# A transformer block on one core: weight splits in short steps, compressed logits joined to the window's, gates kept as inverses

## The chip, the cores and the metric

The kernel runs on one core of a Trainium2 chip. The metric is the device time of one execution in microseconds (us). A core has TensorE (PE in the profile), VectorE (DVE), ScalarE (ACT), GpSimd (POOL) and SyncE (SP), which issues most DMAs; POOL issues others. Each engine works through its own list of instructions in a fixed order, and semaphores tie the lists together.

## The reference

One block on x of 1024 positions by 1024 features, all in float32. Cut to what matters here:

```python
u = rms_norm(h, g_norm_mix)
proj = u @ w_in + b_in            # mLSTM q, k, v, o, i, f; NSA q, 6 x kv, gates; merge gates
y_m = mlstm_mixer(...)            # 4 heads of 128, chunks of 128
# NSA: 8 heads of 64 in 2 groups, queries in blocks
kc_, vc_ = compress(k_c, 0), compress(v_c, 1)          # 63 compressed keys and values per group
p_c = masked_softmax(q @ kc_.T + bias_c, cmp_end <= t)
p_s = masked_softmax(q @ k_sel.T + bias_s, mask_s)     # 16 blocks of 64: here all of them
p_w = masked_softmax(q @ k_win.T + bias_w, window 512)
y_n = gate_c * (p_c @ vc_) + gate_s * (p_s @ v_sel) + gate_w * (p_w @ v_win)
mixed = sum(sigmoid(merge) * einsum('btnw,nwd->btnd', [y_m, y_n], w_branch))
h = h + mixed @ w_out
h = h + (silu(f @ w_gate) * (f @ w_up)) @ w_down       # f = rms_norm(h, g_norm_ffn)
out = rms_norm(h, g_final)
```

With 1024 positions the 16 selected blocks are all blocks, so the selected branch is causal attention over all keys. The gates are the sigmoids of three columns per head.

## The kernel before, in words

A float32 product is made of three PE matmuls on a high and a low part of each factor (`mm3`, L269 to L272): high times high (L270), weight low times input high or the reverse (L271, L272). A tensor is split by ACT, which writes the rounded high part, and by DVE or POOL, which writes the difference, the low part. `Stream.split` (L236 to L251) does that for a weight tile of 128 x 8 x 128: ACT's copy is L247, the subtraction L249, on POOL where `pool` is set, else on DVE.

The program runs in stages. Up to about 80 us the input is normalised and transposed and the first projections are made. From there to about 318 the mLSTM runs beside dense projections. From 318 to 382 the query projections of NSA are made (`b2_dense`), two halves to a tile: ACT evicts a half (L846, `snq`), DVE rounds it (L847, `hnq`) and takes the low part (L848, `lnq`), and SP writes both to memory (L850, L851, `d_qh` and `d_ql`). Beside them `compress` makes the 63 compressed keys and values per group; its weights are loaded at L877 (SP), its features come from DVE (L883), its matmuls are L887. After the first query tile `load_pair(0)` has POOL load the queries of a pair of heads (L810, L811) and the keys of a group in high and low parts (L818 to L821: `KH`, `KL`, index 1 for the window's, 0 for the selected keys), 128 x 1024 each, and SP the bias tables `FB`, `FW`.

From 382 to 707 the attention runs in 32 units: 4 pairs of heads by 8 blocks of 128 query rows, in the order 0, 7, 1, 6, 2, 5, 3, 4 of the blocks i. A unit has five logit jobs (`s_job`, L942): window of head 0 and 1 ("w"), compressed of both heads ("c"), selected of head 0 and 1 ("s"). A job takes one of two PSUM buffers S, runs its matmuls with the queries as weights (L974, L975; for "c" L960, L961 with 8i + 8 columns), then DVE adds the bias and keeps the row maximum (L987, with a readout into `nx`), which frees the buffer, and ACT takes the exponential with the row sum (L991, into `E..`). POOL clears the masked part of `Ec` (L956). `scale` then makes the factor gate / sum in three small DVE operations (L1003 to L1005, `rs`) and multiplies the probabilities (L1013); PE transposes them in groups (L1043, `T`), ACT and DVE split the result (L1048 `TH`, L1052 `TL`), and PE multiplies with the values (L1063, L1065).

The order in this stage is made by a list scheduler at build time: each operation has a cost in ns, a queue (PE, ACT, DVE) and dependencies, and the operation that can start first goes next. Where PE would wait, it places three matmuls of the first nine merge-gate tiles (`merge_tile`, "d" in the trace), whose weights POOL splits. From 707 to 870 come the other merge tiles and the branch products, then w_out and the feed-forward network, which has its own scheduler and isn't touched.

The kernel keeps gates in `GT` as sigmoids, and the buffer counts that the change touches are: low part and staging of the queries ("sl", "st") two each, merge staging ("mg") two, attention output ("os") three.

Of the kernel before, what the change touches and what calls it, by code (L numbers as in the profile page):

```python
# [14 lines left out]
P = 128  # L15
T = 1024
# [15 lines left out]
FX = 1152  # L32
NEG = -1.0e30
# [8 lines left out]
def cast32(ap):  # L42
    return ap.bitcast(F32)
# [114 lines left out]
def body(ctx, tc, a, out, stop=None, dbg=None):  # L158
# [51 lines left out]
    class Stream:  # L210
# [131 lines left out]
    with ExitStack() as sa:  # L342
# [222 lines left out]
        def gates():  # L565
# [69 lines left out]
            nc.scalar.activation(GT[:, :, 0:24], GT[:, :, 0:24], AF.Sigmoid)  # L635
            nc.scalar.preload_act_table_set(EXPLN)
# [167 lines left out]

    def load_pair(p):
# [7 lines left out]
        if p % 2 == 0:  # L813
            for j in (1, 0):
                kh = kq.tile([P, T], F32R, name=f"KH{g}{j}", tag=f"KH{j}", bufs=1)
                kl = kq.tile([P, T], F32R, name=f"KL{g}{j}", tag=f"KL{j}", bufs=1)
                gs = slice(64 * g, 64 * g + 64)
                nc.gpsimd.dma_start(kh[0:64, :], d_kh[j][gs, :])  # L818
                nc.gpsimd.dma_start(kh[64:128, :], d_kh[j][gs, :])
                nc.gpsimd.dma_start(kl[0:64, :], d_kl[j][gs, :])  # L820
                nc.gpsimd.dma_start(kl[64:128, :], d_kl[j][gs, :])  # L821
                KS[g, j] = (kh, kl)
        for r in range(2):
            h = 2 * p + r
            f = kq.tile([P, T], F32, name=f"FB{h}", tag=f"FB{r}", bufs=1)
            w = kq.tile([P, 640], F32, name=f"FW{h}", tag=f"FW{r}", bufs=1)
            for t_, o_, n_ in ((f, 127, T), (w, FX + 127, 640)):
                d_ = d_rep[h][0:1, :]
                nc.sync.dma_start(t_, bass.AP(tensor=d_.tensor, offset=d_.offset + o_, ap=[[RW - 1, P], [1, n_]]))
            FB[h], FW[h] = f, w  # L830


    with ExitStack() as sb:
# [73 lines left out]
        driver(b2_dense(), compress())  # L907
        if "VHC" in dbg:
# [9 lines left out]
    def merge_tile(j, sp, psp, bufs, tag="mg", tbufs=2):  # L918
# [8 lines left out]
    with ExitStack() as sc:  # L927
# [14 lines left out]
        def s_job(u, kind, r):  # L942
# [10 lines left out]
            if kind == "c":  # L953
                n8, nn = 8 * i + 8, ncmp(i)
                e = cp.tile([P, 2, P], F32, name=f"E{u}c", tag="Ec", bufs=3)
                nc.gpsimd.memset(e[:, :, nn:P], 0.0)  # L956
                EX[u, "c"] = e
                for q in range(2):
                    o = s[:, 64 * q:64 * q + n8]
# [3 lines left out]
                rows_ = [(e[:, q, 0:nn], s[:, 64 * q:64 * q + nn], FB[2 * p + q][:, y0:y0 + 16 * (nn - 1) + 1:16], q, 0)  # L963
                         for q in range(2)]
                cost = 4 * 107.0
            else:
                b = 1 if kind == "s" else 2
                n, k0 = (P * (i + 1), 0) if b == 1 else (P * nwin(i), P * max(0, i - 4))
                kh, kl = KS[g, b - 1]
                q_ = QA[2 * p + r]  # L970
                cost = 0.0
                for c0 in range(0, n, 512):
                    m = min(512, n - c0)
                    nc.tensor.matmul(s[:, c0:c0 + m], q_[:, cs], kh[:, k0 + c0:k0 + c0 + m], start=True, stop=False)  # L974
# [18 lines left out]
            return cost, low, exp  # L993

        def scale(u, part):
# [36 lines left out]
        def t_job(u, gi, grp, last):  # L1032
# [21 lines left out]
            def pv():  # L1054
# [11 lines left out]
                if last:  # L1066
                    os_ = cp.tile([P, 256], F32, name=f"os{u}", tag="os", bufs=3)
# [38 lines left out]
        def build_s(u):  # L1106
            p, i = units[u]
            ops = {}
            for k, r in (("w", 0), ("w", 1), ("c", 0), ("s", 0), ("s", 1)):
                b = {"w": 2, "c": 0, "s": 1}[k]  # L1110
                box = {}

                def emit(u=u, k=k, r=r, box=box):
                    _, box["low"], box["exp"] = s_job(u, k, r)

                n = 126 if k == "c" else (P * (i + 1) if b == 1 else P * nwin(i))
                cost = 428.0 if k == "c" else 2 * sum(max(107.0, min(512, n - c) / 2.4) for c in range(0, n, 512))
# [10 lines left out]
                nr = 2 if k == "c" else 1  # L1128
                tt = push(Op("DVE", nr * (80.0 + 1.044 * (n / nr)), [so], lambda box=box: box["low"](), (u, 1)))
                s_free.append(tt)  # L1130
                ex = push(Op("ACT", nr * (290.0 + 0.833 * (n / nr)), [tt], lambda box=box: box["exp"](), (u, 1)))
                ops[k, r] = ex
                if k == "c" or (k == "s" and r == 1):
                    part = 0 if k == "c" else 1
                    de = [ops["w", 0], ops["w", 1], ex] if part == 0 else [ops["s", 0], ex]
                    todo = scale(u, part)
                    rs = push(Op("DVE", 600.0, de, todo[0][0], (u, 2)))
# [106 lines left out]
        todo_pair = {p: sum(1 for u in range(NU) if units[u][0] == p) * 5 for p in range(4)}  # L1244
# [675 lines left out]
```

## Time and profile before

| | |
|---|---|
| median of 3 runs | 1622.4 us (1619.43 to 1623.4) |
| profiled execution | 1624.57 us, span 1622.8 us |
| mean granted TensorE clock | 0.991 |
| busy PE / DVE / ACT / POOL | 1572.2 / 1066.4 / 746.6 / 204.5 us |
| chain that ended last | PE 82%, DVE 4%, DMA 3% |

Busy times are sums over the span; the shares differ from stage to stage, so the stretches are read one by one. A granted clock of 1.00 is 2.4 GHz, 0.50 is 1.2 GHz. An idle time is shown with the instruction that ended it. Matmuls overlap in the records, so their pitch is the distance from start to start, not the duration shown.

### The profile page before, as it was taken

To read this page: it belongs to the slowest core of one execution; us is meant where nothing else is said; L and a number is where in the kernel's file an instruction comes from. 1 tells how busy PE (TensorE), PEld (TensorE's weight loads), DVE (VectorE), ACT (ScalarE), POOL (GpSimd) and SP (SyncE) were. 2 spreads that over 40 slices of the span, in tenths; PEclk is the share of its full clock that TensorE was granted. 3 is DMA by queue.
4 is the path that set the end of the run, shared out by engine and by line. 5 is a ranking of instruction groups with operands and counts; after the bars stand their busy time and mean duration, and the time that the engine had idled before them with its cause. 6 is when DMAs were issued, how large, how long until landed. Compare 5 with 4: busy or idle time off the path is not lost.

```text
span 1622.8 us, 22113 instructions
## 1 busy us (share of the span) xinstructions
PE 1572.2 (97%) x7938; PEld 1327.5 (82%) x7938; DVE 1066.4 (66%) x2276; ACT 746.6 (46%) x1561; POOL 204.5 (13%) x225
## 2 busy tenths in 40 slices
PE   6999999989999999999999998999999999999997
PEld 6876888878989888988887887888888888888876
DVE  6456553245888687952355378666676666978996
ACT  5225455325878687853334344333333333454443
POOL 4002333310102110012000014000000000000130
PEclk9999999999999999999999999999999999999999
DMA  8003532782233422154447222222332223741202
GB/s 251 7 22 97 150 116 96 240 242 70 67 101 82 125 66 82 40 173 148 143 139 255 74 85 85 78 87 89 118 103 78 79 78 104 285 166 42 98 7 104
DMA packets 143773, 181.43 MB, mean 112 GB/s; under 512 B 10414, under 2 KB 100944, under 8 KB 143664
## 3 DMA queue, kind: packets, MB, share of 16 engines
q1 hardware_dynamic: 137440, 157.31, 31.5%
q0 software_dynamic: 5888, 22.06, 4.8%
q8 instruction: 62, 1.02, 0.3%
q10 hardware_dynamic: 336, 0.66, 0.1%
q14 instruction: 47, 0.39, 0.1%
HBM read 137.95 MB, written 49.90 MB: 116 GB/s over the span
## 4 chain that ended last, share of the span: by engine, by line
PE 82%; DVE 4%; DMA 3%; ACT 1%; issue 1%; SPq 0%; POOL 0%; DVEq 0%; ACTq 0%
PE PS L271 14%; PE PS L272 14%; PE PS L270 14%; PE d L270 6%; PE d L272 6%; PE d L271 6%; PE T L1043 4%; PE obank L1063 2%; PE obank L1065 2%; PE br L270 1%; PE br L271 1%; PE br L272 1%; DMA raw<-in_w_in 1%; PE pn L696 1%; DMA q<-d_yn 0%
## 5 line engine op out<-in xcount | busy, mean ns | idle before, releaser
L270 PE MATMUL d<-UTH,whi 128*128 128x512 f32 x576 | 235.1, 408 | 3.4 <-ACT snq L846 2.4
L272 PE MATMUL d<-UTH,wlo 128*128 128x512 f32 x576 | 227.1, 394 | 1.1 <-POOL wlo L249 1.1
L271 PE MATMUL d<-UTL,whi 128*128 128x512 f32 x576 | 226.1, 393 | 0.0
L1421 DVE TENSOR_TENSOR sl<-PS,sl 128x512 f32<-128x512 f32 x182 | 124.0, 688 | 100.2 <-PE PS L272 98.4
L272 PEld LDWEIGHTS d<-UTH,wlo 128*128 128x128 f32 x576 | 108.9, 189 | 26.1 <-POOL wlo L249 1.9
L270 PEld LDWEIGHTS d<-UTH,whi 128*128 128x128 f32 x576 | 109.2, 190 | 21.9 <-ACT snq L846 3.0
L249 POOL TENSOR_TENSOR wlo<-raw,whi 128x1024 fp32r<-128x1024 f32 x31 | 76.2, 2458 | 402.5 <-ACT whi L247 308.2
L271 PEld LDWEIGHTS d<-UTL,whi 128*128 128x128 f32 x576 | 109.6, 190 | 17.6
L1052 DVE TENSOR_TENSOR TL<-T,TH 128x512 fp32r<-128x512 f32 (+1 forms) x184 | 103.7, 583 | 20.9 <-ACT TH L1048 19.5
L1048 ACT ACTIVATE TH<-T 128x512 fp32r<-128x512 f32 (+1 forms) x184 | 90.8, 511 | 34.4 <-PE T L1043 31.6
L1421 DVE TENSOR_TENSOR sl<-sl,sl 128x512 f32<-128x512 f32 (+1 forms) x113 | 77.3, 691 | 18.3 <-ACT sl L1424 12.9
L1424 ACT ACTIVATE sl<-sl 128x512 f32<-128x512 f32 (+1 forms) x85 | 53.5, 631 | 69.8 <-PE PS L271 47.6
L1063 PE MATMUL obank<-TH,VHL 128*128 128x256 f32 x264 | 76.4, 312 | 0.0
L1424 ACT ACTIVATE wh<-sl 128x512 fp32r<-128x512 f32 x61 | 38.5, 631 | 81.9 <-PE PS L271 71.6
L1421 POOL TENSOR_TENSOR acc<-acc 128x512 f32<-128x512 f32 x6 | 9.2, 1548 | 503.5 <-DVE acc L1421 503.4
L1065 PE MATMUL obank<-TL,VHL 128*128 128x256 f32 x264 | 68.5, 282 | 0.0
L270 PE MATMUL PS<-q 128*128 128x512 f32 x172 | 66.9, 389 | 0.0
L271 PE MATMUL PS<-q 128*128 128x512 f32 x172 | 66.9, 389 | 0.0
L272 PE MATMUL PS<-q 128*128 128x512 f32 x172 | 66.9, 389 | 0.0
L1383 DVE TENSOR_TENSOR q<-br,q 128x512 f32<-128x512 f32 x32 | 21.9, 688 | 67.3 <-ACT q L1376 47.0
L1424 ACT ACTIVATE q<-sl 128x512 fp32r<-128x512 f32 x74 | 43.4, 624 | 46.5 <-PE PS L271 29.1
L1421 DVE TENSOR_TENSOR q<-sl,q 128x512 fp32r<-128x512 f32 x72 | 50.3, 736 | 2.9 <-ACT q L1424 2.9
(1418 smaller groups left out, 4302.0 us busy)
## 6 DMA issues: line engine op xcount, KB each, us to landing
raw<-in_w_in SPq DMA_DIRECT2D x40, 512.0 KB, 4.7
ra<-in_w_gate SPq DMA_DIRECT2D x22, 512.0 KB, 5.3
d_gu<-sl SPq DMA_DIRECT2D x44, 256.0 KB, 2.1
q<-d_mg SPq DMA_DIRECT2D x32, 256.0 KB, 3.2
d_rep<-d_row POOLq DMA_DIRECT2D x8, 960.0 KB, 10.0
sl<-d_gu SPq DMA_DIRECT2D x15, 512.0 KB, 5.3
sl<-in_w_down SPq DMA_DIRECT2D x15, 512.0 KB, 5.2
ra<-in_w_up SPq DMA_DIRECT2D x11, 512.0 KB, 3.8
```

Source lines behind the costliest of these rows:

```text
L249: eng.tensor_tensor(lo, v, cast32(hi), ALU.subtract)
L270: nc.tensor.matmul(ps, ah, bh, start=first, stop=False)
L271: nc.tensor.matmul(ps, ah, bl, start=False, stop=False)
L272: nc.tensor.matmul(ps, al, bh, start=False, stop=last)
L1043: nc.tensor.transpose(pt[:, z, P * r:P * r + P], e, ident)
L1048: nc.scalar.activation(hl[0][:, 0:m], pt[:, 0:m], AF.Copy)
L1052: nc.vector.tensor_tensor(hl[1][:, 0:m], pt[:, 0:m], cast32(hl[0])[:, 0:m], ALU.subtract)
L1063: nc.tensor.matmul(po, vv, th[:, z, :], start=(st[1] == 0), stop=False)
L1065: nc.tensor.matmul(po, vv, tl[:, z, :], start=False, stop=(st[1] == st[2]))
L1383: nc.vector.tensor_tensor(sg[b], ps, sg[b], ALU.mult)
L1421: return pl.step(alts, lambda e: ENG[e].tensor_tensor(out_(), x(), y(), alu), reads, writes, **kw)
L1424: return pl.step((("ACT", cost),), lambda e: nc.scalar.activation(out_(), x(), fn), reads, writes, **kw)
```

## The change

Four things are changed, and planner costs with them.

1. `Stream.split` on POOL is done in steps of two of the eight blocks of a tile: four instructions of 128 x 256 instead of one of 128 x 1024.
2. The tiles of the window keys get 64 more columns behind each block of 128. `behind` has POOL copy the group's compressed keys there. The last window block's matmul then has 192 columns and gives the compressed logits too; the job "c" is gone, and its bias, maximum and exponential become part of the two window jobs. For blocks i of 1 to 3 the window is made by two matmul pairs instead of one. The window keys are loaded block by block, 512 bytes at a time instead of 4096.
3. `GT` is turned into its reciprocal once, and the factor becomes 1 / (max(sum, 1e-30) * (1 / gate)): two small operations instead of three.
4. "sl", "st" and stage C's "mg" have one buffer instead of two, "os" two instead of three. Costs in the scheduler: a matmul max(109, columns / 2.4 + 13) instead of max(107, columns / 2.4), `rs` 400 instead of 600, jobs four to a unit instead of five.

```diff
@@ Stream.split
-                eng = nc.gpsimd if pool else nc.vector
-                eng.tensor_tensor(lo, v, cast32(hi), ALU.subtract)
+                if pool:
+                    m = v.shape[1]
+                    for z in range(0, m, 2):
+                        zs = slice(z, min(m, z + 2))
+                        nc.gpsimd.tensor_tensor(lo[:, zs], v[:, zs], cast32(hi)[:, zs], ALU.subtract)
+                else:
+                    nc.vector.tensor_tensor(lo, v, cast32(hi), ALU.subtract)
@@ gates
+            nc.vector.reciprocal(GT[:, :, 0:24], GT[:, :, 0:24])
@@ before load_pair
+    def behind(g):
+        for t_, c_ in zip(KS[g, 1], (KHC, KLC)):
+            nc.gpsimd.tensor_copy(t_[:, :, P:KB], c_[:, g, None, :].to_broadcast([P, NT, KB - P]))
@@ load_pair
-                kh = kq.tile([P, T], F32R, name=f"KH{g}{j}", tag=f"KH{j}", bufs=1)
...
-                nc.gpsimd.dma_start(kh[0:64, :], d_kh[j][gs, :])
...
+                m = KB if j == 1 else P
+                kh = kq.tile([P, NT, m], F32R, name=f"KH{g}{j}", tag=f"KH{j}", bufs=1)
...
+                        nc.gpsimd.dma_start(t_[64 * z:64 * z + 64, :, 0:P], d_[j][gs, :].rearrange("p (b c) -> p b c", c=P))
...
+            if g > 0:
+                behind(g)
@@ b2_dense.evict
-                    lo = bp.tile([P, 512], F32R, name=f"l{nm}{j}{half}", tag="sl", bufs=2)
-                    st = bp.tile([P, 512], F32, name=f"s{nm}{j}{half}", tag="st", bufs=2)
+                    lo = bp.tile([P, 512], F32R, name=f"l{nm}{j}{half}", tag="sl", bufs=1)
+                    st = bp.tile([P, 512], F32, name=f"s{nm}{j}{half}", tag="st", bufs=1)
@@ after b2_dense and compress
+        behind(0)
@@ s_job
-            if kind == "c":
...
-                    nc.tensor.matmul(o, QA[2 * p + q][:, cs], KHC[:, g, 0:n8], start=True, stop=False)
-                    nc.tensor.matmul(o, QA[2 * p + q][:, cs], KLC[:, g, 0:n8], start=False, stop=True)
...
+                if nw > 1:
+                    logits(s[:, o0:o0 + n - P], lambda k: k[:, i + 1 - nw:i, 0:P], False)
+                logits(s[:, o0 + n - P:o0 + n - P + KB], lambda k: k[:, i, :], True)
...
+                rows_ = [(ec[:, r, 0:nn], s[:, o0 + n:o0 + n + nn], f[:, y0:y0 + 16 * (nn - 1) + 1:16], r, 0)]
@@ scale.first
-                nc.vector.tensor_scalar(rs, sm, 1.0e-30, None, ALU.max)
+                nc.vector.scalar_tensor_tensor(rs, sm, 1.0e-30, gt, ALU.max, ALU.mult)
                 nc.vector.reciprocal(rs, rs)
-                nc.vector.tensor_tensor(rs, rs, gt, ALU.mult)
@@ build_s
-            for k, r in (("w", 0), ("w", 1), ("c", 0), ("s", 0), ("s", 1)):
+            for k, r in (("w", 0), ("w", 1), ("s", 0), ("s", 1)):
```

On PE, in unit 9 (heads 2 and 3, row block 7), the second window job, the transposes of unit 8 behind it and the compressed job stand so before:

```order
L974 MATMUL S9w_4409<-KH_2880,QA_4194 128x512
L975 MATMUL S9w_4409<-KL_2881,QA_4194 128x512
L974 MATMUL S9w_4409<-KH_2880,QA_4194 128x128
L975 MATMUL S9w_4409<-KL_2881,QA_4194 128x128
L1043 MATMUL T_0_4429<-cst,E8w_4353 128x128
L1043 MATMUL T_0_4429<-cst,E8w_4357 128x128
L1043 MATMUL T_1_4432<-cst,E8c 128x128 x2
...
L960 MATMUL S9c_4448<-KHC,QA_4191 128x64
L961 MATMUL S9c_4448<-KLC,QA_4191 128x64
L960 MATMUL S9c_4448<-KHC,QA_4194 128x64
L961 MATMUL S9c_4448<-KLC,QA_4194 128x64
```

After, S9w_4423 and S9w_4450 are the window jobs of the two heads:

```order
L977 MATMUL S9w_4423<-KH_2927,QA_4201 128x512
L978 MATMUL S9w_4423<-KL_2928,QA_4201 128x512
L977 MATMUL S9w_4423<-KH_2927,QA_4201 128x192
L978 MATMUL S9w_4423<-KL_2928,QA_4201 128x192
L1059 MATMUL T_0_4441<-cst,E8w_4363 128x128
L1059 MATMUL T_0_4441<-cst,E8w_4369 128x128
L1059 MATMUL T_1_4444<-cst,E8c 128x128 x2
L977 MATMUL S9w_4450<-KH_2927,QA_4204 128x512
L978 MATMUL S9w_4450<-KL_2928,QA_4204 128x512
L977 MATMUL S9w_4450<-KH_2927,QA_4204 128x192
L978 MATMUL S9w_4450<-KL_2928,QA_4204 128x192
```

The four matmuls of S9c are gone, and the last window pair has 192 columns instead of 128; a group of transposes moves between the two window jobs.

On POOL, the loads of the first group's keys and the first split of the attention stage stand so before (x2: two such instructions in a row):

```order
L818 DMA KH_2880<-d_kh_102 64x1024
L819 DMA KH_2880<-d_kh_102 64x1024
L820 DMA KL_2881<-d_kl_104 64x1024
L821 DMA KL_2881<-d_kl_104 64x1024
L818 DMA KH_2886<-d_kh_101 64x1024
L819 DMA KH_2886<-d_kh_101 64x1024
L820 DMA KL_2887<-d_kl_103 64x1024
L821 DMA KL_2887<-d_kl_103 64x1024
L249 TENSOR_TENSOR wlo_3241<-raw_3109,whi_3240 128x1024
L956 MEMSET E0c 128x2x121
```

After, with the window keys' tiles KH_2927 and KL_2928 loaded in blocks:

```order
L834 DMA KH_2927<-d_kh_102 64x8x128 x2
L834 DMA KL_2928<-d_kl_104 64x8x128 x2
L834 DMA KH_2933<-d_kh_101 64x1024 x2
L834 DMA KL_2934<-d_kl_103 64x1024 x2
L816 COPY KH_2927<-KHC 128x8x64
L816 COPY KL_2928<-KLC 128x8x64
L996 MEMSET E0c 128x121 x2
L254 TENSOR_TENSOR wlo_3294<-raw_3156,whi_3293 128x256 x4
```

The two copies of the compressed keys come in behind the loads, the memsets in halves, and the split in four.

On DVE, the factor of unit 17 and the scaling of its probabilities stand so before:

```order
L1003 TENSOR_SCALAR rs_5583<-sm_5582 128x2x2
L1004 RECIPROCAL rs_5583<-rs_5583 128x2x2
L1005 TENSOR_TENSOR rs_5583<-rs_5583,GT 128x2x2
L1013 TENSOR_SCALAR E17w_5589<-E17w_5589,rs_5583 128x640
L1013 TENSOR_SCALAR E17w_5600<-E17w_5600,rs_5583 128x640
L1013 TENSOR_SCALAR E17c<-E17c,rs_5583 128x63 x2
```

After, with the next unit's first window job behind them:

```order
L1020 SCALAR_TENSOR_TENSOR rs_5576<-sm_5575,GT 128x2x2
L1021 RECIPROCAL rs_5576<-rs_5576 128x2x2
L1029 TENSOR_SCALAR E17w_5578<-E17w_5578,rs_5576 128x640
L1029 TENSOR_SCALAR E17w_5590<-E17w_5590,rs_5576 128x640
L1029 TENSOR_SCALAR E17c<-E17c,rs_5576 128x63 x2
L1004 ISA E18w_5674,nx_5670<-S18w_5673,FB_5334 128x256
L1004 ISA nx_5670 128x1
L1004 ISA E18c,nx_5670<-S18w_5673,FB_5334 128x15
L1004 ISA nx_5670 128x1
L1004 ISA E18w_5702,nx_5670<-S18w_5701,FB_5338 128x256
```

The product with GT is gone from between the reciprocal and the scaling, and each window job now has two bias operations with a readout each, E18w and E18c, on the one PSUM tile.

## Rows read from the trace of the kernel before

**Rows 1.** The page, part 1: engines' busy time and share.
```profile
PE 1572.2 (97%) x7938; PEld 1327.5 (82%) x7938; DVE 1066.4 (66%) x2276; ACT 746.6 (46%) x1561; POOL 204.5 (13%) x225
```

**Rows 2.** Stretches: PE, PEld, DVE, ACT, POOL busy; clock, DMA, GB/s.
```profile
318.00:382.00 64.00, 57.85 (x274) 47.63 (x273) 22.71 (x58) 13.95 (x20) 9.30 (x15) 0.92 0.68 192
382.00:707.00 325.00, 318.14 (x2121) 285.37 (x2119) 270.36 (x904) 256.55 (x675) 38.29 (x61) 1.00 0.30 76
```

**Rows 3.** PE's waits, whole span: total us, times, longest us.
```profile
PE d L272 <- POOL wlo L249: 1.1, 2, 0.7
...
PE S25s L974 <- DVE nx L987: 0.7, 1, 0.7
```

**Rows 4.** PE's timeline at 465: start, duration, operation, idle before.
```profile
465.82 0.30 PE L960 MATMUL S9c<-KHC,QA 128*128 128x64 f32 x1 [0.21 <-DVE nx L987]
...
466.29 0.44 PE L1043 MATMUL T<-cst,E8s 128*128 128x128 f32 x2
...
467.50 0.28 PE L1063 MATMUL obank<-TH,VHC 128*128 128x256 f32 x1
...
467.73 0.39 PE L974 MATMUL S9s<-KH,QA 128*128 128x512 f32 x1
...
468.19 0.40 PE L974 MATMUL S9s<-KH,QA 128*128 128x512 f32 x1
```

**Rows 5.** PE's timeline in unit 0, at 384 us.
```profile
384.07 0.17 PE L960 MATMUL S0c<-KHC,QA 128*128 128x8 f32 x1
...
384.44 0.31 PE L974 MATMUL S0s<-KH,QA 128*128 128x128 f32 x1
```

**Rows 6.** POOL, DVE and PE timeline, attention, 555 and 594 us.
```profile
555.74 2.41 POOL L249 TENSOR_TENSOR wlo<-raw,whi 128x1024 fp32r<-128x1024 f32 x1 [19.55 <-ACT whi L247]
...
556.41 2.16 DVE L1003 TENSOR_SCALAR rs<-sm 128x4 f32<-128x4 f32 x1
...
559.62 0.33 PE L1043 MATMUL T<-cst,E17w 128*128 128x128 f32 x1 [1.17 <-DVE E17w L1013]
...
594.92 2.37 DVE L1005 TENSOR_TENSOR rs<-rs,GT 128x4 f32<-128x4 f32 x1
...
598.38 0.33 PE L1043 MATMUL T<-cst,E20s 128*128 128x128 f32 x1 [1.54 <-DVE TL L1052]
```

**Rows 7.** Groups by line, POOL: count, busy us, mean ns, idle before.
```profile
L249 POOL TENSOR_TENSOR wlo<-raw,whi 128x1024 fp32r<-128x1024 f32 x31 | 76.2, 2458 | 402.5 <-ACT whi L247 308.2 <-DVE lnq L848 34.3 <-PE S12s L975 29.0
...
L1421 POOL TENSOR_TENSOR sl<-sl,sl 128x512 f32<-128x512 f32 x3 | 3.8, 1274 | 37.1 <-ACT sl L1524 37.0
```

**Rows 8.** Groups by line, DVE, attention stage: the product with the gates.
```profile
L1005 DVE TENSOR_TENSOR rs<-rs,GT 128x4 f32<-128x4 f32 x32 | 7.5, 235 | 1.1
```

**Rows 9.** DVE, POOL and PE timeline at 130 us.
```profile
130.04 2.31 DVE L675 COPY dec<-SB 128x8 f32<-128x8 f32 x1 [6.42 <-DMA SB<-d_S]
...
132.29 2.40 POOL L674 TENSOR_TENSOR MB<-cst,MB 128x1024 f32<-128x1024 f32 x1
...
138.78 0.49 PE L696 MATMUL pn<-MV,PT 128*128 128x129 f32 x2 [3.50 <-DVE PT L690]
```

**Rows 10.** PE's timeline between 357 and 365 us.
```profile
357.34 0.50 PE L270 MATMUL d<-UTH,whi 128*128 128x512 f32 x1 [1.94 <-ACT snq L846]
...
364.20 2.05 PE L887 MATMUL ph<-fl,w 128*128 128x126 f32 x8 [3.75 <-DMA w<-in_w_cmp]
```

**Rows 11.** ACT's timeline at 355 us.
```profile
355.48 1.06 ACT L247 ACTIVATE whi<-raw 128x1024 fp32r<-128x1024 f32 x1 [8.90 <-DMA raw<-in_w_in]
```

**Rows 12.** DMA queues, 340 to 348 us: packets, MB, share of 16 engines.
```profile
q0 software_dynamic: 527, 1.71, 87.8%
q1 hardware_dynamic: 598, 0.32, 39.9%
```

**Rows 13.** The tile d_ql, issues from 331 to 346 us: issue to landing.
```profile
DMA to landing us min/median/max: 2.0/11.8/18.7
```

**Rows 14.** The tile E9c on DVE: duration in ns, start.
```profile
L987 DVE CUSTOM_DVE_ANT_0 E9c<-S9c,FB x2: 252/254/255, 467.1 to 467.3; 128x63 f32<-128x63 f32 x2
```

More of the change, by code (lines that the diff above doesn't have):

```diff
@@ L32 @@
 FX = 1152
+KB = 192
 NEG = -1.0e30
@@ new lines, in s_job, with logits @@
+            b = 1 if kind == "s" else 2
+            kh, kl = KS[g, b - 1]
+            q_ = QA[2 * p + r]
+            e = cp.tile([P, T if b == 1 else 640], F32, name=f"E{u}{kind}{r}", tag="E" + kind, bufs=4)
+            EX[u, kind, r] = e
+            f = FB[2 * p + r]
+            def logits(o, k_, last):
+                nc.tensor.matmul(o, q_[:, cs], k_(kh), start=True, stop=False)
+                nc.tensor.matmul(o, q_[:, cs], k_(kl), start=False, stop=True)
+            if b == 1:
+                n, o0 = P * (i + 1), 0
+                for c0 in range(0, i + 1, 4):
+                    m = min(4, i + 1 - c0)
+                    logits(s[:, P * c0:P * (c0 + m)], lambda k: k[:, c0:c0 + m, :], False)
+                rows_ = []
+            else:
+                nw = nwin(i)
+                n, o0 = P * nw, P if nw == 4 else 0
+                if nw > 1:
+                    logits(s[:, o0:o0 + n - P], lambda k: k[:, i + 1 - nw:i, 0:P], False)
+                logits(s[:, o0 + n - P:o0 + n - P + KB], lambda k: k[:, i, :], True)
+                if r == 0:
+                    EX[u, "c"] = cp.tile([P, 2, P], F32, name=f"E{u}c", tag="Ec", bufs=3)
+                ec, nn = EX[u, "c"], ncmp(i)
+                nc.gpsimd.memset(ec[:, r, nn:P], 0.0)
+                y0 = 31 + 16 * (56 - 8 * i)
+                rows_ = [(ec[:, r, 0:nn], s[:, o0 + n:o0 + n + nn], f[:, y0:y0 + 16 * (nn - 1) + 1:16], r, 0)]
@@ L991, in exp @@
                     nc.scalar.activation(e_, e_, AF.Exp, bias=nx[:, q, b:b + 1], scale=-1.0, accum_out=sm[:, q, b:b + 1])
-            return cost, low, exp
+            return low, exp
         def scale(u, part):
@@ L1108, in build_s @@
             ops = {}
-            for k, r in (("w", 0), ("w", 1), ("c", 0), ("s", 0), ("s", 1)):
-                b = {"w": 2, "c": 0, "s": 1}[k]
+            for k, r in (("w", 0), ("w", 1), ("s", 0), ("s", 1)):
+                b = {"w": 2, "s": 1}[k]
                 box = {}
                 def emit(u=u, k=k, r=r, box=box):
-                    _, box["low"], box["exp"] = s_job(u, k, r)
-                n = 126 if k == "c" else (P * (i + 1) if b == 1 else P * nwin(i))
-                cost = 428.0 if k == "c" else 2 * sum(max(107.0, min(512, n - c) / 2.4) for c in range(0, n, 512))
+                    box["low"], box["exp"] = s_job(u, k, r)
+                if b == 1:
+                    n, parts = P * (i + 1), [min(512, P * (i + 1) - c) for c in range(0, P * (i + 1), 512)]
+                else:
+                    n, parts = P * nwin(i), [P * (nwin(i) - 1)] * (nwin(i) > 1) + [KB]
+                cost = 2 * sum(max(109.0, m / 2.4 + 13.0) for m in parts)
                 deps = []
@@ L1127, in build_s @@
                 chain["S"] = [so]
-                nr = 2 if k == "c" else 1
-                tt = push(Op("DVE", nr * (80.0 + 1.044 * (n / nr)), [so], lambda box=box: box["low"](), (u, 1)))
+                nr, n = (2, n + ncmp(i)) if b == 2 else (1, n)
+                tt = push(Op("DVE", nr * 180.0 + 1.044 * n, [so], lambda box=box: box["low"](), (u, 1)))
                 s_free.append(tt)
-                ex = push(Op("ACT", nr * (290.0 + 0.833 * (n / nr)), [tt], lambda box=box: box["exp"](), (u, 1)))
+                ex = push(Op("ACT", nr * 290.0 + 0.833 * n, [tt], lambda box=box: box["exp"](), (u, 1)))
                 ops[k, r] = ex
-                if k == "c" or (k == "s" and r == 1):
-                    part = 0 if k == "c" else 1
-                    de = [ops["w", 0], ops["w", 1], ex] if part == 0 else [ops["s", 0], ex]
+                if r == 1:
+                    part = 0 if k == "w" else 1
+                    de = [ops[k, 0], ex]
                     todo = scale(u, part)
-                    rs = push(Op("DVE", 600.0, de, todo[0][0], (u, 2)))
+                    rs = push(Op("DVE", 400.0, de, todo[0][0], (u, 2)))
                     bl = [2, 2, 0, 0] if part == 0 else [1, 1]
@@ L1242, in place_dense @@
             dstate["gate"] = gate
-        todo_pair = {p: sum(1 for u in range(NU) if units[u][0] == p) * 5 for p in range(4)}
+        todo_pair = {p: sum(1 for u in range(NU) if units[u][0] == p) * 4 for p in range(4)}
         pair_at[0] = 2500.0
```

40 lines of the change are left out of this document (7 added, 33 removed).

## The prediction

> **What bounds the kernel now.** I read the busy times of the page first: TensorE (PE) works for 97% of the span, VectorE (DVE) for 66%, ScalarE 46%, GpSimd (POOL) 13% [rows 1]. A gain therefore has to take time from PE: its matmuls, its idle time, or its clock. The busy times by stage come next [rows 2]. In the attention stage (382 to 707 us), where most of the edits lie, PE is busy 318.14 of 325.00 us with the full clock granted, while DVE has 325.00 - 270.36 = 55 us to spare and ScalarE 68. So operations saved on DVE there are worth nothing by themselves, and PE matmuls saved are worth their pitch. In the stage before it (318 to 382), PE is idle 64.00 - 57.85 = 6.1 us and the mean granted clock is 0.92. The sums of PE's waits say which stalls GpSimd and the logit buffers cause [rows 3], and the timelines what stands around them.
>
> My sum is made against the profiled execution, 1624.57 us (span 1622.8), which lies 2.2 above the median of the runs, 1622.4.
>
> **Joined compressed logits.** Removed are four matmuls per unit (two heads, a high and a low part), 128 in 32 units. In unit 9 four start at 465.82 and the next work at 466.29: 0.47 [rows 4]. In unit 0, with 8 columns instead of 64, it is 384.44 - 384.07 = 0.37 [rows 5], so width hardly counts. The sum is 32 x 0.42 = 13.4 us; bounds 32 x 0.37 = 11.8 and 32 x 0.47 = 15.0. Added: the last window block's pair has 192 columns instead of 128. The trace has no 192. Its nearest rows are two c matmuls, 0.47 / 2 = 0.23, and two of 256 columns, 467.73 - 467.50 = 0.23 [rows 4]; a 192 pair lies between, so it costs no more than the 128 pair that it replaces in row blocks 0 and 4 to 7. In row blocks 1 to 3 there were no separate last blocks: one pair of 256, 384 or 512 columns becomes two. With 0.23 for 256, 0.46 for 512 (468.19 - 467.73) and 0.35 for 384 as their middle, the extra is 0.23, then 0.23 + 0.23 - 0.35 = 0.11, then 0.35 + 0.23 - 0.46 = 0.12. Each comes 8 times (2 heads, 4 pairs): 3.7 us, 3.4 to 4.2 if a pair is off by 0.02. Net -9.7 us, between -7.6 and -11.6.
>
> The Trainium skill (TensorE: Matmul & The Clock Gate, Back-to-back issue gap) gives about 81 ns per 128-column matmul in a stream of weight load and matmul. By that 128 x 0.081 would go and 48 x 0.081 come, -6.5. The rows have 0.09 to 0.12 per small matmul, and the measurement decides.
>
> **Splits in four steps.** The long split is 2.458 us x 31 and a GpSimd operation of half its width 1.274 [rows 7]. That is 2.31 ns per column and 0.09 fixed, so 256 columns take about 0.68, four 2.7: +0.3 us of GpSimd per tile, on an engine with 87% free. What counts is who is held meanwhile. At 555.74 the split starts, and DVE's rs operation on 4 elements, begun at 556.41, takes 2.16 us, where such an operation has a mean of 0.235 [rows 8]; it ends just behind the split, and PE then waits 1.17 us at 559.62 for what DVE scales with it. At 594.92 another takes 2.37, and PE waits 1.54 at 598.38 [rows 6]. With steps such an operation can be held for one step: at 130.04 DVE's copy was held for 2.31 and was served when the split ended, although the next GpSimd operation began at 132.29 right behind [rows 9]. So a hold falls from up to 2.4 to 0.7, and of the 2.7 us of PE time in these two places I take -2.5 off, bounds -3.5 (smaller places too) and 0 (a hold in another place for each one cured). PE's own waits for the low parts of the weights are 1.1 us in two places, 0.7 the longest [rows 3]; the steps let the first k-blocks start earlier: -0.7. The other one lies ahead of the gap of 3.50 at 138.78 [rows 9], which ends when a chain of DVE and GpSimd work ends. That chain is as long in four steps as in one; the time saved ahead is lost in it: 0, bounds -4 and +1.
>
> **Inverse gates.** One DVE operation less in each of 64 calls, 0.235 us each for the larger half [rows 8], about 13 us of DVE work, and one reciprocal more in an earlier stage. DVE has the 55 us of slack, so 0; it shortens the chain to the first transposed group of a unit, by 0.2 where PE waits for that. If PE's waits were all on DVE this would be worth up to 2 us.
>
> **Fewer buffers, loads in other pieces, the new order.** The query tiles' low part and staging have one buffer instead of two. The next low part must now wait until the last one has landed in memory: 2.0 to 18.7 us after its issue [rows 13]. Behind it on DVE stand the next weight split and the compression's features, behind it on SP's queue the compression's weights, for which PE waits 3.75 at 364.20 [rows 10]. Against that, half of the window keys' load now moves in 512-byte pieces. At 340 to 348 the two queues moved 527 packets with 1.71 MB and 598 packets with 0.32 MB [rows 12]: about one for one, so the queue with the small packets (SP's) got a sixth of the bytes. With smaller packets on the other side SP's transfers land sooner: the weight tile for which ScalarE waited 8.90 at 355.48, and which held back the evictions for which PE waited 1.94 at 357.34 [rows 10, 11], and the low parts. At best both PE gaps go, 5.7, and with them the stretch of half clock (1.2 GHz) behind them: 0.92 over 64 us is 5.1 us short, some 2.8 of it outside the gaps, 8.5 in all. At worst landings stay as they are, and the wait puts 2.4 more into the gap at 364.20 and up to 1.6 of half clock: +4. I take -4, the side of the packet counts, at half of their reach.
>
> The Trainium skill (DMA: Bandwidth & Descriptors, Queues, rings and completion order) says that an engine drains a packet of some 9 to 17 descriptors from one ring before it turns to the next. By that, pieces of 512 bytes would travel in groups and SP's queue would gain little. No run here shows GpSimd's queue with small pieces; this is the first rival.
>
> The attention stage's order changes with fewer jobs and other costs, and the merge tiles' filler runs out earlier at its end; single buffers for staging and outputs add short waits: +1, between -1 and +4. GpSimd's copies of the compressed keys, two of 512 columns at about 1.3 [rows 7], stand before the first logits and, for the second group, in a stretch where the keys land microseconds ahead of use: 0, or up to 2.6 if that cover is gone.
>
> **Sum:** -9.7 - 2.5 - 0.7 + 0 - 4 + 1 = -15.9: 1608.7 as profiled, 1606.5 as a median. I say 1607.
>
> **Rivals.** (a) The single buffers decide in the stage before attention, and small pieces do not help: +3 there instead of -4, so 1613.5. For it: landings up to 18.7 us; against: the packet counts. (b) All of that stage's gaps close: -8.5 instead of -4, 1602. (c) PE time saved turns into idle time, because DVE's and ScalarE's chain per unit, not PE, sets the pace when 10 us of PE work are gone: then the stage takes as long, and only -2.5 - 0.7 in stalls is won, offset by new ones: about 1620. Against: the slack of 55 and 68 us. (d) Slower: a joined job holds one of the two logit buffers for a second DVE read. That read takes 0.254 [rows 14]; with its readout, about 0.34. If each of 64 window jobs makes PE wait that long, 22 us are added against 15.9 saved: 1628.5. It decides from 0.25 us per job. Against: PE's longest wait for such a buffer is 0.7 us now [rows 3], and the removed job held a buffer as well.
>
> **Chances.** Forecast 0.45, (a) 0.23, (b) 0.18, (c) 0.08, (d) 0.04; the rest small mixes. The forecast's cases, (a) and (b) are all faster by over 0.3% (4.9 us, about what a measurement of this kernel can tell from no change): with the rest 0.89. Within it 0.07, slower 0.04. The range from 1599 to 1617 takes in (b) and (a) with 3 us for the run-to-run spread and the sum's bounds.
>
> **What would show it.** In the attention stage PE's busy time falls by about 10 us and the stage by 11 to 13; no DVE operation on a few elements takes over 1 us beside a split; the waits for TL and E17w fall below 0.7 each; PE no longer waits for the split in the merge stage. Before it, the weight tile that ScalarE got at 355.48 lands before 350, and PE's gap of 1.94 goes; (a) shows instead as DVE idle until a query's low part has landed and a gap over 3.75 for the compression's weights. (c) shows as PE idle in the attention stage grown by 8 us or more, (d) as waits of logit matmuls for nx of many microseconds. I am wrong if the time is above 1617, where the saved matmuls did not leave PE's path.

## The result: 1604.85 us, 1.0% faster, by other terms than those of the sum

The changed kernel took 1604.85 us (median of 5 runs, 1604.28 to 1606.35) against 1622.52 for the kernel before in the same runs: ratio 0.9896, 95% interval 0.9882 to 0.9909. The forecast of 1607 holds, and the two largest gains forecast beside the matmuls do not: of the gains only the first term of the sum has its size, and errors in the other terms made up for each other.

The busy times of the changed kernel's page, which answer to [rows 1], and its stretches in the columns of [rows 2]:

```profile
PE 1558.8 (97%) x7858; PEld 1317.6 (82%) x7858; DVE 1046.7 (65%) x2214; ACT 742.3 (46%) x1560; POOL 230.7 (14%) x355
```
```profile
318.00:382.00 64.00, 57.87 (x282) 48.45 (x281) 23.21 (x68) 14.80 (x27) 14.40 (x26) 0.95 0.78 199
382.00:707.00 325.00, 321.50 (x2101) 287.16 (x2100) 260.45 (x839) 258.53 (x680) 48.95 (x120) 1.00 0.35 86
```

The last row ends 17 us behind the changed stage's end, so stages are compared here between their own bounds. A stage is counted between starts of PE's matmuls in the trace: the mLSTM and query stages from the first `pn` matmul (one of the mLSTM's), which began at 138.78 before [rows 9], to the first matmul behind the compression's last, and the attention from there to the first matmul behind the last `obank` (the products with the values). The attention of before and of after, by the same view:

```profile
380.08:707.16 327.08, 320.06 (x2129) 286.98 (x2129) 271.66 (x907) 258.61 (x678) 39.02 (x61) 1.00 0.30 76
```
```profile
377.10:689.79 312.69, 309.19 (x2049) 277.08 (x2049) 256.83 (x844) 254.04 (x677) 46.21 (x120) 1.00 0.33 79
```

327.08 - 312.69 = 14.39 us less, of which 320.06 - 309.19 = 10.87 is PE's work and 3.52 its idle time. In the distances from each matmul's start to the next (idle time apart), the 128 compressed logits had 13.33 us; the window logits went from 31.15 (192 matmuls) to 35.21 (240). The other four kinds of matmul, unchanged in number, lost 1.6 together; why is not shown. One window job of unit 9:

```profile
457.60 0.48 PE L977 MATMUL S9w<-KH,QA 128*128 128x512 f32 x1
...
458.15 0.25 PE L977 MATMUL S9w<-KH,QA 128*128 128x192 f32 x1
...
458.35 0.42 PE L277 MATMUL d<-UTH,whi 128*128 128x512 f32 x1
```

The pair of 192 columns takes 458.35 - 458.15 = 0.20 us, no more than the 0.23 of its neighbours in [rows 4]. The waits of PE and the splits on GpSimd:

```profile
PE ph L902 <- DVE lnq L863: 5.7, 1, 5.7
...
PE T L1059 <- DVE TL L1068: 1.7, 4, 0.6
...
PE obank L1081 <- DVE TL L1068: 0.4, 1, 0.4
```
```profile
L254 POOL TENSOR_TENSOR wlo<-raw,whi 128x256 fp32r<-128x256 f32 x124 | 96.6, 808 | 323.7 <-ACT whi L248 289.9 <-DVE TL L1068 16.4 <-DVE nx L1004 13.9
```

The wait for a `wlo` split is gone from the list and no wait for `nx` is in it. PE's worst new wait, 5.7 us, stands ahead of the attention, at the first matmuls of the compression (`ph`). A step takes 0.81 us on average (an estimate of 0.68 had stood for it), four 3.2 instead of 2.46. Around that wait:

```profile
346.32 1.06 ACT L248 ACTIVATE whi<-raw 128x1024 fp32r<-128x1024 f32 x1 [1.65 <-DMA raw<-in_w_in]
...
355.68 0.69 DVE L863 TENSOR_TENSOR lnq<-snq,hnq 128x512 fp32r<-128x512 f32 x1 [4.94 <-DMA d_ql<-lnq]
356.29 3.84 DVE L898 TENSOR_SCALAR fl<-KX,COLS 128x126 f32<-128x126 f32 x16
...
356.77 1.17 SPq L892 DMA_DIRECT2D w<-in_w_cmp  x2
...
361.20 2.04 PE L902 MATMUL ph<-fl,w 128*128 128x126 f32 x8 [5.68 <-DVE lnq L863]
```

The weight tile that ScalarE got at 355.48 before [rows 11] is there at 346.32, and the gap of 1.94 behind it is gone. The wait ahead of the compression has grown from 3.75 [rows 10] to 5.68, so PE is idle there as long as before (1.94 + 3.75 = 5.69). The profile names a query's low part as what ended it; e7 and e11 below speak for the weights.

### The profile page after: what moved, and what is told of

It reads as the page before. It is cut to its first block, busy times and chain, and to the rows that moved or that the text cites. A ratio compares the mean times of both kernels' runs of the same rounds, so it can differ in the third digit from the quotient of the medians.

```text
span 1602.6 us, 21999 instructions
## 1 busy us (share of the span) xinstructions
PE 1558.8 (97%) x7858; PEld 1317.6 (82%) x7858; DVE 1046.7 (65%) x2214; ACT 742.3 (46%) x1560; POOL 230.7 (14%) x355
## 3 DMA queue, kind: packets, MB, share of 16 engines
q0 software_dynamic: 9472, 22.06, 5.5%
q8 instruction: 62, 1.02, 0.3%
## 4 chain that ended last, share of the span: by engine, by line
PE 85%; DVE 3%; DMA 2%; ACT 1%; issue 0%; POOL 0%; SPq 0%; DVEq 0%; ACTq 0%
PE PS L278 15%; PE PS L279 15%; PE PS L277 15%; PE d L277 7%; PE d L279 7%; PE d L278 7%; PE T L1059 4%; PE obank L1081 2%; PE obank L1079 2%; PE br L278 1%; PE br L277 1%; PE br L279 1%; DMA d_ql<-lnq 1%; PE pn L704 1%; DMA raw<-in_w_out 0%; PE pa L692 0%
## 5 line engine op out<-in xcount | busy, mean ns | idle before, releaser
L254 POOL TENSOR_TENSOR wlo<-raw,whi 128x256 fp32r<-128x256 f32 x124 | 96.6, 808 | 323.7 <-ACT whi L248 289.9
```

The costliest lines, as they stand in the source:

```text
L254: nc.gpsimd.tensor_tensor(lo[:, zs], v[:, zs], cast32(hi)[:, zs], ALU.subtract)
```

## The experiments

All ratios are to the kernel before, timed beside.

| kernel | median us | ratio, 95% interval | pn to attention | attention (PE idle) |
|---|---|---|---|---|
| before | 1622.52 | | 241.30 | 327.08 (7.02) |
| changed | 1604.85 | 0.9896 (0.9882 to 0.9909) | 239.50 | 312.69 (3.50) |
| e1 before, steps | 1619.05 | 0.9979 (0.9970 to 0.9988) | 238.20 | 326.12 (5.99) |
| e2 changed, splits in one instruction | 1606.92 | 0.9903 (0.9888 to 0.9918) | 240.92 | 312.82 (3.50) |
| e3 join, buffer cuts, costs | 1609.13 | 0.9920 (0.9906 to 0.9934) | 240.11 | 315.10 (4.57) |
| e4 before, gates | 1619.90 | 0.9984 (0.9975 to 0.9993) | 240.75 | 325.08 (5.57) |
| e5 before, buffer cuts | 1624.76 | 1.0016 (1.0006 to 1.0025) | 244.25 | 327.22 (7.09) |
| e6 e5 and pieces | 1621.96 | 0.9992 (0.9983 to 1.0000) | 240.55 | 327.00 (6.99) |
| e7 changed, low part in place | 1605.74 | 0.9893 (0.9880 to 0.9906) | 240.14 | 312.77 (3.51) |
| e8 changed, steps ahead only | 1605.68 | 0.9898 (0.9884 to 0.9912) | 240.19 | 312.72 (3.50) |
| e9 changed, weights early | 1598.81 | 0.9854 (0.9837 to 0.9870) | 233.20 | 312.71 (3.49) |
| e10 e7 and e9 | 1597.93 | 0.9844 (0.9828 to 0.9861) | 231.81 | 312.68 (3.50) |
| e11 changed again | 1606.02 | 0.9894 (0.9879 to 0.9909) | 238.07 | 312.67 (3.51) |

Stage lengths are from the one profiled execution. The attention's length repeats within 0.25 us where its order is the same (before, e5, e6; changed, e2, e7 to e11), the stage ahead of it only within 1.5 (changed and e11).

**e1, the steps alone**, on the kernel before:

```diff
-                eng = nc.gpsimd if pool else nc.vector
+                if pool:
+                    m = v.shape[1]
+                    for z in range(0, m, 2):
...
```

> The kernel before with the splits on GpSimd in four steps and nothing else. Theory (a DVE operation is held only for one step): in the attention stage no DVE operation on a few elements takes over 1 us beside a split, PE's idle time there falls from 7.0 us by 2.5 to 3.5, and PE's wait of 0.67 for a split in the merge stage goes: -3.5 us, about 1619. [...] Rival (the holds only move elsewhere, and GpSimd is busy longer): within 1 us of the kernel before, 1622.

-3.7 us, as the first theory had it in sum, and PE's wait for a split in the merge stage is gone, but the attention gave 0.96 (idle time 1.03) instead of 2.5 to 3.5. The rest lies outside the attention and is not placed. At the first of the two places of [rows 6]:

```profile
552.01 3.09 POOL L253 TENSOR_TENSOR wlo<-raw,whi 128x256 fp32r<-128x256 f32 x4 [19.09 <-ACT whi L247]
...
552.68 0.17 DVE L1009 TENSOR_SCALAR rs<-sm 128x4 f32<-128x4 f32 x1
...
552.89 0.18 DVE L1010 RECIPROCAL rs<-rs 128x4 f32<-128x4 f32 x1
...
553.10 0.38 DVE L1011 TENSOR_TENSOR rs<-rs,GT 128x4 f32<-128x4 f32 x1
...
553.51 2.31 DVE L1019 TENSOR_SCALAR E17w<-E17w,rs 128x640 f32<-128x640 f32 x2
...
555.88 0.98 PE L1049 MATMUL T<-cst,E17w 128*128 128x128 f32 x7 [0.99 <-DVE E17w L1019]
```

The operations on four elements are no longer stuck (0.17, 0.18, 0.38). Now the next ones are: two scalings of E17w take 2.31 us, where the two had taken 1.02 in the kernel before. They run beside the third and fourth step of the same tile, and PE waits 0.99 instead of 1.17. At the second place of [rows 6] the wait of 1.54 falls to 0.22 and 0.49; at 462.12 a wait for `nx` is 0.61, 0.21 before. Counting DVE's operations that stand beside a split and take over 0.3 us more than the median of their kind, the attention has three in the kernel before, 5.4 us over in sum, and eight in e1, 4.8 us over: short steps shorten each hold here and hardly the sum of the holds.

**e2, the changed kernel with the split in one instruction**, the same edit undone.

> The changed kernel with the splits on GpSimd in one instruction again. Theory: operations of DVE on a few elements of over 1.5 us come back beside the splits, with PE's waits behind them: +3 to +4 us, about 1608.5. Rival (with the order of the changed kernel the long splits happen to hold nothing): 1605, within 1 us of the changed kernel.

1606.92: in between, 2 and 1 us above the changed kernel's two medians (1604.85 and 1606.02), and nothing of it in the attention:

```profile
L250 POOL TENSOR_TENSOR wlo<-raw,whi 128x1024 fp32r<-128x1024 f32 x31 | 76.3, 2461 | 335.5 <-ACT whi L248 298.3 <-DVE TL L1062 16.8 <-DVE nx L998 14.0
...
L1014 DVE SCALAR_TENSOR_TENSOR rs<-sm,GT 128x4 f32<-128x4 f32 x32 | 5.1, 160 | 2.7 <-ACT E20c L1002 0.9 <-ACT E29c L1002 0.7 <-ACT E27c L1002 0.4
```
```profile
379.81:692.63 312.82, 309.32 (x2048) 277.07 (x2048) 256.84 (x844) 254.17 (x677) 42.54 (x93) 1.00 0.34 79
```

The three views are the groups of GpSimd, those of DVE and the stage's row. The long splits are back, the factor's first operation has a mean of 0.160 us in its group, so not one of the 32 was held, and the stage takes 312.82. The first theory is wrong for this stage. In the changed order no operation on the factor begins beside one of the stage's nine splits; in the order before three did, and all three were held. What DVE does beside the splits in e2 reads a PSUM tile and takes its usual time: TL at 526.05 took 0.69 beside a split of 2.40. In the attention, in each of these traces, every held operation (the factor, the scaling of `E`) has its data outside PSUM, in SBUF, the core's other memory.

The 1 to 2 us in the whole are at the edge of what the runs tell: the intervals of e2 and of the changed kernel overlap.

**e3, the join without steps and gates**: e2 with the three operations for the factor back.

> The changed kernel with one-instruction splits and with gates as before (three small operations for the factor), so that only the joined logits, their keys' layout and the buffer cuts are left of the change. Theory (the join and what comes with it carry most of the gain): PE's logit matmuls of the attention stage take 9.3 us less than before, the stage before it 3 us less, the whole about 1609 to 1610. Rival (the gates carry 3 us or more, since PE waits on the chain through the factor): 1612 or more.

Left of the change are the joined logits, the keys' layout, the buffer cuts and the scheduler's costs; among these is one that the list of the change leaves out, the fixed cost of a bias operation, 180 ns instead of 80.

1609.13, the first theory in sum; the stage ahead of the attention is 1.2 us shorter, not 3. The attention's row:

```profile
379.10:694.20 315.10, 310.53 (x2048) 276.62 (x2049) 265.37 (x908) 255.13 (x677) 42.45 (x93) 1.00 0.33 79
```

315.10, so the join and the order that comes with it take 11.98 off: PE's work -9.53, idle -2.45. Cuts and layout have no part in it (327.22 and 327.00 in e5 and e6); no run has the new costs without the join, so whose the 2.45 are is not shown. No DVE operation is held beside a split here, though the splits are in one instruction. The gates then take 315.10 - 312.82 = 2.28.

**e4, the gates alone**: on the kernel before, the reciprocal in the earlier stage and

```diff
-                nc.vector.tensor_scalar(rs, sm, 1.0e-30, None, ALU.max)
+                nc.vector.scalar_tensor_tensor(rs, sm, 1.0e-30, gt, ALU.max, ALU.mult)
                 nc.vector.reciprocal(rs, rs)
-                nc.vector.tensor_tensor(rs, rs, gt, ALU.mult)
```

> The kernel before with the gates kept as inverses and nothing else. Theory (DVE has 55 us of slack in the attention stage, and one small operation less is off PE's path): DVE busy -13 us, time within 1.5 us of the kernel before, 1621 to 1623. Rival (the factor's chain is on PE's path wherever PE waits for a scaled tile): -3 us, 1619.5.

-2.85, nearer the rival (the interval runs from -1.1 to -4.1). The attention, and PE at the place that had cost 1.17:

```profile
378.60:703.68 325.08, 319.51 (x2128) 287.24 (x2129) 262.25 (x843) 258.00 (x678) 39.00 (x61) 1.00 0.30 76
```
```profile
557.04 1.23 PE L1043 MATMUL T<-cst,E17w 128*128 128x128 f32 x6 [0.59 <-DVE E17w L1013]
```

DVE's busy time falls by 271.66 - 262.25 = 9.4 us, and the stage by 2.00, idle 7.02 to 5.57. Of the 0.58 us that PE waits less at this place, some 0.2 is the operation that is gone (0.17 and the step to the next); the rest is a shorter hold, for the factor's first operation takes 1.78 beside the split instead of 2.16. Three operations are held here too, 5.0 us over in sum. That the gates are worth 2 us without any hold is shown by e3 against e2, 2.28, of which 1.07 is idle time; the rest is PE's work, and why it falls is not shown.

**e5, the buffer cuts alone**: "sl", "st", "mg" at one, "os" at two, on the kernel before.

> The kernel before with the four buffer cuts alone (query low part and staging one, merge staging one, attention output two). Theory (the low part must wait for the landing of the last one): DVE waits for a landing of d_ql, SP issues the compression's weights 2 us or more later than at 359.46, and the stage before the attention gets 2 to 4 us longer: 1625. Rival (the wait is covered, since PE has other work): within 1 us, 1622.5.

+2.4 us, the theory's size (the stage +2.95), by another wait of PE's than that for the weights:

```profile
356.05 1.06 ACT L247 ACTIVATE whi<-raw 128x1024 fp32r<-128x1024 f32 x1 [10.00 <-DMA raw<-in_w_in]
...
357.41 0.69 DVE L848 TENSOR_TENSOR lnq<-snq,hnq 128x512 fp32r<-128x512 f32 x1 [12.48 <-DMA d_ql<-lnq]
...
358.95 0.79 PE L270 MATMUL d<-UTH,whi 128*128 128x512 f32 x1 [4.08 <-ACT snq L846]
...
361.57 1.18 SPq L877 DMA_DIRECT2D w<-in_w_cmp  x2
...
366.76 2.05 PE L887 MATMUL ph<-fl,w 128*128 128x126 f32 x8 [3.60 <-DMA w<-in_w_cmp]
```

DVE waits 12.48 us until a low part has landed. The weights' issue slips from 359.46 to 361.57 and PE's start on them from 364.20 [rows 10] to 366.76, but its wait there does not grow (3.60, 3.75 before). What grows is the wait ahead of it, for the eviction that stands behind that low part: 4.08 at 358.95, 1.94 before; and half the clock is granted for 13.7 us there instead of 10.2.

**e6, e5 with the window keys in pieces of 512 bytes**, tiles with 64 columns left empty, no join.

```diff
-                nc.gpsimd.dma_start(kh[0:64, :], d_kh[j][gs, :])
+                        nc.gpsimd.dma_start(t_[64 * z:64 * z + 64, :, 0:P], d_[j][gs, :].rearrange("p (b c) -> p b c", c=P))
```

> The last kernel, and the window keys in the tiles with 64 empty columns behind each block of 128, loaded in pieces of 512 bytes; no joined logits. Theory (queues share by packets, so smaller packets on GpSimd's queue let SP's through): the weight tile that ScalarE got at 355.48 in the kernel before is there by 348, PE's wait for snq goes, and the stage before the attention is 3 to 6 us shorter than with the buffer cuts alone: 1620. Rival (an engine drains a packet of many pieces before it turns): the tile lands within 2 us of 355, and the time is that of the buffer cuts, 1625.

-2.8 us against e5, less than the theory's 5 but on its side (the stage 3.7 shorter); in sum with the buffer cuts 0 (-0.4 of the kernel before, and its interval ends at 1). In the same eight us as [rows 12]:

```profile
q0 software_dynamic: 1347, 1.20, 71.2%
q1 hardware_dynamic: 1188, 0.96, 62.6%
```
```profile
348.26 1.06 ACT L248 ACTIVATE whi<-raw 128x1024 fp32r<-128x1024 f32 x1 [1.85 <-DMA raw<-in_w_in]
...
363.25 2.04 PE L888 MATMUL ph<-fl,w 128*128 128x126 f32 x8 [5.98 <-DVE lnq L849]
```

GpSimd's queue moved 1347 packets for 1.20 MB instead of 527 for 1.71, SP's three times its bytes, and ScalarE had the weight tile at 348.26 instead of 355.48 [rows 11]. PE's wait for snq is gone; the one ahead of the compression is 5.98, against 4.08 + 3.60 in e5. By these rows small packets give way, if not one for one each time (2081 to 892 in the changed kernel). The prediction drew from the Trainium skill (DMA: Bandwidth & Descriptors, Queues, rings and completion order), by which a queue's turn is a packet of some 9 to 17 descriptors, that SP's queue would gain little. That did not come, but it does not follow from the rule either: a turn counted in descriptors carries fewer bytes when the pieces are smaller. How many pieces a turn holds no run here shows.

**e7, the low part in place**, two tiles, the memory of the changed kernel:

```diff
-                    lo = bp.tile([P, 512], F32R, name=f"l{nm}{j}{half}", tag="sl", bufs=1)
-                    st = bp.tile([P, 512], F32, name=f"s{nm}{j}{half}", tag="st", bufs=1)
+                    lo = bp.tile([P, 512], F32R, name=f"l{nm}{j}{half}", tag="sl", bufs=2)
+                    st = cast32(lo)
```

> The changed kernel with the queries' low part written over their staging tile, two such tiles: the same memory as in the changed kernel, but a low part need not wait until the last one has landed. Theory (the landing of d_ql holds DVE, and behind it SP's issue of the compression's weights): DVE's two waits of 4.9 us for d_ql go, PE's gap of 5.68 at 361.20 falls below 3, and the stage is 3 to 5 us shorter: 1600.5. Rival (the gap is set by something else, such as the features on DVE or the weights' own transfer in a full queue): within 1.5 us of the changed kernel, 1604 to 1606.

1605.74, the rival:

```profile
350.63 3.98 DVE L898 TENSOR_SCALAR fl<-KX,COLS 128x126 f32<-128x126 f32 x16
...
351.10 3.68 SPq L892 DMA_DIRECT2D w<-in_w_cmp  x2
...
361.02 2.04 PE L902 MATMUL ph<-fl,w 128*128 128x126 f32 x8 [5.77 <-DMA w<-in_w_cmp]
```

DVE no longer waits for a landing (ScalarE's evictions do, 0.23 and 5.84 us), makes the features at 350.63 instead of 356.29, and SP issues the weights at 351.10 instead of 356.77. They land no sooner, 9.8 us after the issue instead of 4.3: PE starts at 361.02, 361.20 in the changed kernel. So the low part alone did not hold the gap, though the changed kernel's trace names it as the releaser; the same kernel's second trace (e11) names the weights, with 5.79. Why the landing takes longer here no run shows.

**e8, the steps in the mLSTM stage only**, the merge tiles' splits in one.

> The changed kernel with the four steps in the mLSTM stage alone; the merge tiles' splits, in the attention stage and behind it, are one instruction. Theory (in the changed order the long splits hold nothing in the attention stage, where one-step and four-step splits took 312.82 and 312.69 us; the 2 us that the steps are worth lie before it): within 1 us of the changed kernel, 1604 to 1606. Rival (the steps gain in the attention or merge stage): 1606.9, as with one-instruction splits everywhere.

1605.68, within the theory's bound, though the single runs (1604.88 to 1609.63) take in the rival's 1606.9 too. The traces are clearer: from PE's first matmul to the first `pn`, kernels with steps there took 127.31 to 127.89 us (e1, e7 to e11, changed), those without 128.00 to 128.45 (before, e2 to e6), 0.66 in the mean. Of it 0.40 is PE's wait for a split near 132 us, which is there in every kernel without the steps and in none with them. The rest of the 2 us is not placed.

**e9, the weights early.** The first of the two weight tiles for the values is loaded 47 us earlier, into the third of the three buffers, free until then:

```diff
+                if j == 0:
+                    yield 4000.0
+                    early = [w1_load(1, 0)]
+                    yield 8000.0
```

> The changed kernel with one edit: of the compression's two weight tiles for the values, the first is loaded some 45 us earlier, into the buffer that stands free. Theory (after the changes PE's gap of 5.7 us ends when the weights have landed, and with the weights there earlier DVE's features end it): PE waits for the features behind the low part (DVE, about 360.1) and then starts: gap 4.5 to 5, stage 1 us shorter, total 1604. Rival (the transfers share bandwidth, and with less to load at that point the low part lands sooner too): gap below 3.5, stage 3 us shorter, 1602.

1598.81, beyond the rival: 6.0 and 7.2 us under the changed kernel's two medians.

```profile
310.05 1.77 SPq L889 DMA_DIRECT2D w<-in_w_cmp  x1
...
356.94 3.95 DVE L904 TENSOR_SCALAR fl<-KX,COLS 128x126 f32<-128x126 f32 x16
...
357.32 1.21 PE L908 MATMUL ph<-fl,w 128*128 128x126 f32 x8 [0.95 <-DVE fl L904]
```

The wait of 5.7 is 0.95, and the half clock behind it is gone too: from 352 to 375 us the mean granted clock is 1.00, 0.85 in the changed kernel. PE starts on the first features (from 356.94 on DVE) as they come; I had let it wait for the sixteenth.

**e10, e7 and e9 together.**

> The changed kernel with both: the low part in place in two tiles (no wait for its landing on DVE) and the first of the two weight tiles loaded early. Theory (two walls stand one behind the other, the landing of the low part and that of the weights, and each edit alone leaves the other): the features end on DVE at about 354.6, the weights are there, PE's gap of 5.7 goes nearly whole (below 1), with it most of the half clock behind it: stage 6 to 8 us shorter, total 1598. Rival (a third wall at about 360, the eviction of the query tile or the second weight tile): gap 3 or more, 1602 to 1604.

1597.93, the theory; the lowest time of all, 0.9844 of the kernel before, though not clearly below e9 (1594.71 to 1598.84 and 1598.21 to 1599.42). Ahead of the compression's matmuls no gap is left. The same stretch in the changed kernel and here:

```profile
352.00:375.00 23.00, 17.32 (x83) 14.60 (x82) 7.73 (x22) 2.66 (x4) 0.55 (x2) 0.85 0.62 180
```
```profile
352.00:375.00 23.00, 22.06 (x120) 18.62 (x119) 8.72 (x30) 7.39 (x17) 3.58 (x10) 1.00 0.69 197
```

PE works 22.06 of 23 us instead of 17.32, and at the full clock instead of a mean of 0.85.

**e11, the changed kernel again**, beside the last two.

> The changed kernel once more, beside the last two, as their yardstick on this chip: 1604 to 1606, the stage before the attention 239 to 241 us from the first mLSTM chunk to its end.

1606.02, as expected but for the stage's 238.07, a little under the least: half the clock was granted for 6.8 us of it, for 10.0 in the first profile.

## Why the prediction was right in sum and wrong in parts

- **Joined logits, -9.7:** right. 13.33 went (13.4 forecast), 35.21 - 31.15 = 4.06 came (3.7), -9.27. The 0.09 to 0.12 per small matmul of the rows held, not the 81 ns of the Trainium skill (TensorE: Matmul & The Clock Gate, Back-to-back issue gap), by which -6.5 was worked out: 13.33 / 128 = 0.104.
- **The holds beside the splits, -2.5:** the step that failed. The holds did go and the idle time fell by 3.52, but not by the steps: with one-instruction splits it is the same 3.50 (e2), and steps alone took 1.03 of it (e1). I took the holds for a property of the split; they were one of the order, three of nine splits that met an operation they could hold. e1 shows also that the bound of one step per hold was read too narrowly, since the next operation is held in its place. What the steps gain in the changed kernel lies outside the attention, 1 to 2 us by the medians. The -0.7 for the wait in the merge stage was not theirs alone: that wait was gone in e2, e3 and e4 too, without steps. Ahead of the gap at 138.78, where the sum had 0, the steps bring the first `pn` 0.66 sooner (e8).
- **Inverse gates, 0:** wrong, 2.0 to 2.3 in the stage and 2.85 timed by themselves. The slack of 55 us was an average; the chain sums, factor, scaled tile, transpose ends PE's waits at single places, such as 1.17 at 559.62 [rows 6], 0.59 in e4. That bound (2 us) stood in the text and was not taken.
- **Single buffers and small pieces, -4:** both mechanisms there, +2.4 (e5) and -2.8 (e6), so the net is near nothing, -0.4 timed. The small pieces closed the gap of 1.94, and the gap ahead of the compression grew by as much (3.75 to 5.68). The mistake was to let both gaps go together: with the low part out of the way (e7) the second stayed, and it closed when the weights were loaded early (e9). Of the stretch at half clock, 10.2 us, 3.75 lay in that gap, so 3.2 us were lost outside the gaps, not 2.8.
- **The new order, +1:** wrong in sign. Join and new costs together take 2.45 us of PE's idle time off (e3). The three waits behind held operations, 1.17, 1.54 and 0.41, are not in e3; whether fewer jobs or other costs moved them is open.
- **Rivals.** Ahead of the attention the signs of the forecast (the weight tile at 346.32, the gap of 1.94 gone) and those of (a) (DVE idle for 4.94 until a low part has landed, a gap over 3.75) came together. (b) did not occur; its closed gaps came only with the weights loaded early. (c) and (d) did not occur: idle fell, and no wait for `nx` is in the list.

That the sum came out is in part luck: the profiled attention is 14.4 us shorter where the sum had 11.2, and the stage ahead of it 1.8 (3.2 in e11) where it had 4. The parts timed apart (e1, e4, e3) come to -3.7 - 2.85 - 13.6 = -20.2, the whole to -17.7, a difference that their intervals leave open; in the attention's lengths the parts come to 0.96 + 2.00 + 11.98 = 14.94 against 14.39, so little was counted twice there.

## What to carry to other kernels

A held instruction is a meeting of two instructions in one order. Before counting a gain from shortening the long ones, look how many of them met one that can be held (in the attention before, three of nine, and only operations without PSUM data), and what stands behind it. Slack of an engine over a stage says nothing on a chain that PE waits for at single places. When a gap's named releaser is removed and the gap stays, look for a second arrival close by: load early what has a free buffer, then look again.

## What the hardware showed that was not expected

The clock does not always fall behind a gap of PE. In the kernel before the gap of 3.50 that ended at 138.78 [rows 9] and one of 2.20 that ended at 873.85 were followed by half the clock; in e1 gaps of 3.34 and 2.92 at the same places were not. The rows, in the columns of [rows 2]:

```profile
141.00:143.00 2.00, 2.00 (x6) 1.55 (x5) 2.00 (x1) 0.00 (x0) 2.00 (x1) 0.50 0.00 0
...
874.20:877.50 3.30, 3.30 (x9) 2.65 (x8) 2.35 (x4) 1.75 (x3) 0.00 (x0) 0.50 0.40 68
```
```profile
137.00:146.00 9.00, 8.27 (x41) 6.26 (x42) 8.66 (x17) 4.28 (x11) 3.25 (x4) 1.00 0.22 60
...
868.50:876.00 7.50, 7.50 (x33) 6.18 (x34) 5.49 (x6) 3.59 (x4) 0.00 (x0) 1.00 0.67 216
```

One kernel shows both, too: in the changed kernel's first trace half the clock was granted from 137.7 to 140.7, right after a gap of 3.32, and in its second (e11) the full clock, after one of 3.67. A stretch of 3.3 us at 1.2 GHz, as in the second row, costs half its length (an estimate: the work would take half as long at 2.4 GHz), so one profile against another carries that much chance; the attention, where the full clock is granted, repeats within 0.25 us.
